# Hybrid decoder trunk: weight items of the up projection in two rings, each in the SBUF half of its operand

## The chip, the cores and the metric

The kernel runs on one core of one Trainium2 chip. The metric is the device time of one execution in microseconds. Engines are named as the profile names them: PE is TensorE (PEld its weight loads), DVE is VectorE, ACT is ScalarE, POOL is GpSimd, SP is SyncE.

## What is computed

Two layers over 1024 tokens of width 1024, all in fp32. Each layer has a token mixer of three parallel groups (latent attention, gated linear attention, RWKV-7) and a gated feed-forward part:

```python
for l in range(2):
    p = rms_norm(x) @ w_in
    y = concat[MLA(p_a), GLA(p_b), RWKV7(p_c)]            # width 1024
    x = x + y @ w_out
    u = rms_norm(x) @ w_up                                # 1024 -> 2 x 2816
    u = causal depthwise conv of width 3 over tokens (u) + bias
    gate, val = u[:, :2816], u[:, 2816:]
    x = x + (silu(gate) * val) @ w_down                   # 2816 -> 1024
out = rms_norm(x)
```

## The kernel before

**Products.** Every fp32 operand is split into two fp32r halves: hi is a copy on ACT, lo is the operand minus hi. One product of matrices is three matmuls (`mm3`, L99 to L102, all recorded at L97): hi by hi, hi by lo, lo by hi.

**Up projection.** The 2816 gate and 2816 value columns are taken in 22 blocks j of 128 each. A block is computed by a scheme of seven products instead of eight (p = 1, 2, 6, 5, 3, 7, 4 in this order, `seq`). Each product has four steps of `mm3`, so 12 matmuls of 128x512: the stationary operand is a weight item ("wr" in the profile: [128, 2, 4, 128], hi and lo, 4 KiB per partition), the moving one an activation operand of 512 tokens: B11 (p=1), B21 (2), B22 (3), T1 (5), T2 (6), T3 (7), T4 (4), 16 KiB per partition each. `rhs` picks it.

**Weight items.** `up_item` makes one item: for p=6 first four sums S of raw weights ("wu") on POOL, X and Y (L1364 to L1367), then `split`: the hi on ACT (L1271), the lo (L1272) on DVE for p = 2, 5, 7, 4 and on POOL for 1, 6, 3. Items lie in RING, seven slots; after product n item n+7 is made. A slot is written when the product that read it is done; a sum is overwritten when its readers are done.

**Evacuation.** `evac` takes a product out of PSUM (four banks, so product n needs the bank of n-4): p=1 and p=5 by ACT, the others by DVE (L1458 for p=2, L1460 for 6, L1465 for 3, L1479 for 7, L1471 for 4), with additions on POOL (L1466 gate, L1480 value). Then the convolution's taps: one on ACT (L1441), two on DVE (L1443), for gate and value; silu on ACT (L1468), the product of the two on DVE (L1475) and the store to `fdr`.

**SBUF.** Tiles are taken from two ends. The left end has the pool `slots` (m0 to m9, kb.., va.., sg, each 4 KiB; its names stand behind the tile's name in the profile, wr_m, T_kb), above 16 KiB of transfer scratch and the constants. The right end has the pools `wp` (ws, wh, wl), in the attention stage those of its tiles (v, p and others), later `xr` (x, raw) and `bp` (the five operands B11, B21, T2, T1, B22). T3 lies in `wp`. So before the change all weight items and T4 lie left, the six other operands right. A tile that takes the bytes of earlier tiles waits for their users.

**Output projection.** y is multiplied by w_out in eight k blocks, whose weights `wout_w` (L1158 to L1171) loads into "wos", splits by ACT (L1170) and, for k above 3, POOL (L1171). k=5, 6, 7 are split last; k=5 and 6 have slots of the left pool, k=7 has `wp`. The buffer of "wos" for these three is `wp`'s ws, two of them. The matmuls of a token tile go over k = 0 to 7. `up_norm` then makes the operands of the up projection for each of eight token tiles i.

**Down projection.** Its operands are loaded into the bytes of the up projection's operands (HOME) by `down_load`, from product p=1 of the last block on, and split into UNITS, nine pairs of buffers, by ACT and DVE.

**Order.** The program's order is that of the Python code, with background generators advanced by `spend`; the tile scheduler then orders each engine's queue by what is ready first in its own time line.

Of the kernel before, what the change touches and what calls it, by code (L numbers as in the profile page):

```python
# [10 lines left out]
F32 = mybir.dt.float32  # L11
F32R = mybir.dt.float32r
AF = mybir.ActivationFunctionType
ALU = mybir.AluOpType
# [47 lines left out]
def trunk(ctx: ExitStack, tc: tile.TileContext, A, out, offs):  # L62
# [241 lines left out]
    for l in range(DEPTH):  # L304
# [838 lines left out]
        def pv(h, i, pT, sm):  # L1143
            po = aps()
            for j in range(i + 1):
# [8 lines left out]
        WOA = (("m6", "m7"), ("m8", "m2"), ("m0", "m1"), ("va00", "va10"), ("kb00", "kb10"), ("kb01", "kb11"),  # L1154
               ("va01", "va11"))
        YA = (("m4", "m5"), ("sg", "m9"))

        def wout_w(k, ws=None):  # L1158
            if k < 7:
                woh[k], wol[k] = (slot(o, [128, D], F32R, "wo") for o in WOA[k])  # L1160
            else:
                woh[7], wol[7] = (wp.tile([128, D], F32R, tag="wl", name="wo7") for _ in range(2))
# [88 lines left out]
        bp = right.enter_context(tc.tile_pool(name=f"bp{l}", bufs=1, side="right", reuse_waits="tile"))  # L1251
        WU, WD = A["ffn_w_up"][l], A["ffn_w_down"][l]
# [8 lines left out]
        B11, B21, T2, T1, B22 = (pair(n) for n in ("B11", "B21", "T2", "T1", "B22"))  # L1261
# [11 lines left out]

        def up_norm(xt, i):
            raw = xr.tile([128, 8, 128], F32, tag="raw", name="raw")
# [25 lines left out]
            if i < 4:  # L1301
                split(at(B11), lo, dve)
                yield
                split(at(B21), hi, pool)
            else:
                for q in at(B11):
                    dve.tensor_tensor(lo, lo, q.bitcast(F32), ALU.subtract)
# [6 lines left out]
                for q in at(B11):  # L1314
                    dve.tensor_tensor(hi, hi, q.bitcast(F32), ALU.subtract)
# [4 lines left out]
        def late_sums():  # L1320
            for n, tags in enumerate((("m1", "kb00"), ("kb10", "kb01"))):
                r = slice(2 * n, 2 * n + 2)
                t = xr.tile([128, 2, 512], F32, tag="raw", name="ts")
# [17 lines left out]
        RING = ("m4", "m5", "sg", "m9", "m8", "kb11", "m3")  # L1341
# [12 lines left out]
        def up_item():  # L1354
            nonlocal rn
            if not todo:
                return
            j, p = todo.pop(0)
            g, v = (wraw[j] + [None])[0:2]
            eng = dve if j < SJ else pool  # L1360
            if p == 6:
                X = slot("va10", [128, 2, 4, 128], F32, "S12")
                Y = slot("va01", [128, 2, 4, 128], F32, "S34")
# [9 lines left out]
            c = slot(RING[rn % len(RING)], [128, 2, 4, 128], F32R, "wr")  # L1373
# [58 lines left out]
        def rhs(p, k):  # L1432
# [3 lines left out]
            a = {1: B11, 2: B21, 3: B22, 5: T1, 6: T2}[p]  # L1436
            return a[0][:, k], a[1][:, k]

        def taps(u, jj, tag):
            a = xr.tile([128, T], F32, **tag, name="acc")  # L1440
# [7 lines left out]
        def evac(j, p):  # L1448
# [3 lines left out]
            if p == 1:  # L1452
                tmp[j] = slot(("va00", "va11")[j % 2], [128, 3, 512], F32, "s")
                act.activation(tmp[j][:, 0], ps, AF.Copy)
# [260 lines left out]
```

## Time and profile before

| | us |
|---|---|
| median of 3 runs | 2757.17 |
| lowest, highest | 2750.89, 2757.83 |
| the profiled execution | 2754.38 |
| its span | 2752.6 |

The span is the stretch from the first to the last instruction in the profile; the profiled execution's own time is 1.8 us more. All times of the trace count from the span's start. Layer 2 follows layer 1 by 1370 us (the first w_out weight of the late three is split at 570.5 and at 1940.5). In layer 1 attention and RWKV last to about 595, the output projection to about 700, the up projection to about 1140, then comes the down projection.

### The profile page before, as it was taken

The page shows a single profiled execution, that of the slowest core. Times are in us where ns is not written, and L with a number is a line of the kernel's source. Part 1 is how long each engine was busy: PE and PEld are TensorE (multiplying, and loading weights), DVE is VectorE, ACT ScalarE, POOL GpSimd, SP SyncE. Part 2 cuts the span into 40 slices and gives each one's busy share as a digit, 9 for nine tenths or more (in the row PEclk, how much of TensorE's full clock was granted, in tenths as well). Part 3 has the DMA queues.
Part 4 walks back from the last instruction along what each step waited for, and adds up shares of the span by engine and source line. Part 5 has one row for each costly group of instructions (what it writes and reads, how often), then busy time and mean ns, then how long its engine had stood idle before and what let it go on. Part 6 is the DMA issues. An engine that isn't in the chain of part 4 may idle for free. (4 is left out here: it accounts for less than half of the span.)

```text
span 2752.6 us, 35450 instructions
## 1 busy us (share of the span) xinstructions
PE 2650.9 (96%) x13586; PEld 2135.5 (78%) x13586; DVE 1867.2 (68%) x2470; ACT 1080.8 (39%) x1764; POOL 1125.0 (41%) x915
## 2 busy tenths in 40 slices
PE   8999999999899999999899999999998999998998
PEld 7668788888778877778786777788887788776786
DVE  3456565645987777888733565555469887878887
ACT  4222244444434344433352223445544444443333
POOL 3446322232676666200134553222327767671001
PEclk9999989999999999999999999899999999999999
DMA  4112221134122222623111122111341222227221
GB/s 128 31 31 62 64 61 38 45 126 138 52 86 77 84 77 77 237 100 101 58 45 31 31 70 73 51 32 57 121 135 54 77 81 81 80 74 260 85 84 62
DMA packets 237050, 224.11 MB, mean 81 GB/s; under 512 B 39288, under 2 KB 187216, under 8 KB 236880
## 3 DMA queue, kind: packets, MB, share of 16 engines
q1 hardware_dynamic: 215104, 211.70, 23.8%
q10 hardware_dynamic: 21008, 8.04, 1.2%
q8 instruction: 107, 1.75, 0.3%
q0 software_dynamic: 768, 2.10, 0.2%
q14 instruction: 63, 0.52, 0.1%
HBM read 166.22 MB, written 53.48 MB: 80 GB/s over the span
## 5 line engine op out<-in xcount | busy, mean ns | idle before, releaser
L97 PE MATMUL psb<-hh,wh 128*128 128x512 f32 (+2 forms) x704 | 267.3, 381 | 6.5 <-ACT acc L748 3.8
L1443 DVE SCALAR_TENSOR_TENSOR acc<-ug,convc,acc 128x1023 f32<-128x1023 f32 x88 | 190.6, 2166 | 122.2 <-ACT acc L1441 122.1
L97 PE MATMUL psb<-hl,wh 128*128 128x512 f32 (+2 forms) x704 | 270.7, 385 | 0.8 <-DVE hl L208 0.8
L97 PE MATMUL psb<-hh,wl 128*128 128x512 f32 (+2 forms) x704 | 270.1, 384 | 0.8 <-POOL wl L258 0.8
L97 PE MATMUL psa<-B,wr_m 128*128 128x512 f32 x744 | 187.7, 402 | 1.9 <-DVE uv L1471 1.9
L97 PE MATMUL psr<-B,wr_m 128*128 128x512 f32 x744 | 185.6, 397 | 0.0
L97 PEld LDWEIGHTS psa<-B,wr_m 128*128 128x128 f32 x744 | 142.6, 192 | 37.5 <-DVE uv L1471 2.7
L254 POOL TENSOR_TENSOR ws<-ws,pcol 128x1024 f32<-128x1024 f32 x36 | 70.4, 1958 | 243.0 <-DMA ws<-in_w_in 242.8
L97 PEld LDWEIGHTS psr<-B,wr_m 128*128 128x128 f32 x744 | 140.6, 189 | 34.2 <-DVE s_va L1460 0.3
L97 PEld LDWEIGHTS psb<-hh,wh 128*128 128x128 f32 (+1 forms) x704 | 132.9, 189 | 36.5 <-issue 4.9
L97 PEld LDWEIGHTS psb<-hh,wl 128*128 128x128 f32 (+1 forms) x704 | 133.2, 189 | 33.3 <-issue 10.5
L97 PEld LDWEIGHTS psb<-hl,wh 128*128 128x128 f32 (+1 forms) x704 | 133.1, 189 | 29.2 <-issue 5.4
L258 POOL TENSOR_TENSOR wl<-ws,wh 128x1024 fp32r<-128x1024 f32 (+1 forms) x40 | 91.0, 2276 | 105.9 <-ACT wh L256 70.9
L1441 ACT ACTIVATE acc<-ug,convc 128x1024 f32<-128x1024 f32 x44 | 54.8, 1246 | 202.1 <-POOL ug L1466 202.1
L1443 DVE SCALAR_TENSOR_TENSOR acc<-uv,convc,acc 128x1023 f32<-128x1023 f32 x88 | 120.0, 1364 | 8.0 <-ACT acc L1441 6.7
L1272 DVE TENSOR_TENSOR wr_m<-wu_m,wr_m 128x512 fp32r<-128x512 f32 x88 | 120.9, 1375 | 0.2 <-ACT wr_m L1271 0.2
L1272 POOL TENSOR_TENSOR wr_sg<-S_va,wr_sg 128x512 fp32r<-128x512 f32 x40 | 58.0, 1449 | 120.0 <-ACT wr_sg L1271 116.3
L1468 ACT ACTIVATE acc<-acc 128x1024 f32<-128x1024 f32 x44 | 46.7, 1062 | 149.1 <-DVE acc L1443 149.1
L1271 ACT ACTIVATE de_m<-R 128x1024 fp32r<-128x1024 f32 x59 | 61.9, 1052 | 109.9 <-PE psb L97 50.8
L1364 POOL TENSOR_TENSOR S_va<-wu_m 128x512 f32<-128x512 f32 x42 | 57.0, 1358 | 114.8 <-issue 107.6
L256 ACT ACTIVATE wh<-ws 128x1024 fp32r<-128x1024 f32 (+2 forms) x44 | 43.7, 993 | 150.7 <-PE psb L97 141.4
L97 PE MATMUL psb<-de 128*128 128x512 f32 x348 | 94.6, 394 | 0.0
(534 smaller groups left out, 7119.0 us busy)
## 6 DMA issues: line engine op xcount, KB each, us to landing
wu_m<-in_ffn_w_up SPq DMA_DIRECT2D x88, 512.0 KB
fdr<-acc SPq DMA_DIRECT2D x44, 512.0 KB
R<-fdr SPq DMA_DIRECT2D x88, 256.0 KB
R<-in_ffn_w_down SPq DMA_DIRECT2D x88, 256.0 KB
ws<-in_w_in SPq DMA_DIRECT2D x38, 512.0 KB
y_m<-ydr SPq DMA_DIRECT2D x16, 512.0 KB
xmid<-x SPq DMA_DIRECT2D x16, 512.0 KB
wos_m<-in_w_out SPq DMA_DIRECT2D x10, 512.0 KB
```

Of the source, the lines that this page charges most:

```text
L97: pe.matmul(o, lhsT=l, rhs=r, start=first, stop=last, skip_group_check=on)
L254: eng.tensor_tensor(ws, ws, g.rearrange("p (k o) -> p k o", o=1).to_broadcast([128, K, M]), ALU.mult)
L256: act.activation(wh, ws, AF.Copy)
L258: eng.tensor_tensor(wl, ws, wh.bitcast(F32), ALU.subtract)
L1271: act.activation(d[0], s, AF.Copy)
L1272: eng.tensor_tensor(d[1], s, d[0].bitcast(F32), ALU.subtract)
L1364: eng.tensor_tensor(X[:, 0], v[:, 0:4], v[:, 4:8], ALU.add)
L1441: act.activation(a, u, AF.Identity, scale=conv[:, 2, jj:jj + 1], bias=conv[:, 3, jj:jj + 1])
L1443: dve.scalar_tensor_tensor(a[:, d:T], u[:, 0:T - d], conv[:, 2 - d, jj:jj + 1], a[:, d:T], ALU.mult, ALU.add)
L1468: act.activation(a, a, AF.Silu)
```

## The change

- Weight items get two rings: three slots on the left (m4, m5, sg) for p=1 and 4, five on the right (RG, 20 KiB in `bp`, at the place where B11 was) for p = 2, 3, 5, 6, 7. `up_item` is called twice after each product and makes an item only if its ring has a free place and at most seven are alive.
- B11 moves to the left: two pieces in kb01, kb11 and va01, va11. T4's second piece takes m3. So every product has weights and activations in the same half.
- Splits of B11 and subtractions of it (`less`) go in two halves of 256 columns each.
- w_out's k=5 and k=6 lose their slots to B11 and use the bytes of RG.
- The transfer scratch goes from 16 to 8 KiB; a pool `lp` (raw, ex) takes the room on the right. The tmp tiles of `evac` and X, Y get other slots on the left.
- Down projection: HOME is B21, T2, T1, B22, RG; the first loads come after p = 2, 6, 5 instead of 1, 2, 6; a tenth unit of operands "e" (raw, ex).

```diff
--- before.py
+++ after.py
@@ -1151,13 +1151,14 @@
         woh, wol, yy = [None] * 8, [None] * 8, {}
-        WOA = (("m6", "m7"), ("m8", "m2"), ("m0", "m1"), ("va00", "va10"), ("kb00", "kb10"), ("kb01", "kb11"),
-               ("va01", "va11"))
+        WOA = (("m6", "m7"), ("m8", "m2"), ("m0", "m1"), ("va00", "va10"), ("kb00", "kb10"))
         YA = (("m4", "m5"), ("sg", "m9"))
         def wout_w(k, ws=None):
-            if k < 7:
+            if k < 5:
                 woh[k], wol[k] = (slot(o, [128, D], F32R, "wo") for o in WOA[k])
+            elif k < 7:
+                woh[k], wol[k] = (RG[:, 2 * k - 10 + n].rearrange("p a k c -> p (a k c)") for n in range(2))
             else:
@@ -1249,6 +1250,7 @@
         bp = right.enter_context(tc.tile_pool(name=f"bp{l}", bufs=1, side="right", reuse_waits="tile"))
+        lp = right.enter_context(tc.tile_pool(name=f"lp{l}", bufs=1, side="right", reuse_waits="tile"))
         WU, WD = A["ffn_w_up"][l], A["ffn_w_down"][l]
@@ -1258,7 +1260,10 @@
 
-        B11, B21, T2, T1, B22 = (pair(n) for n in ("B11", "B21", "T2", "T1", "B22"))
+        RG = bp.tile([128, 5, 2, 4, 128], F32R, tag="RG", name="RG")
+        B21, T2, T1, B22 = (pair(n) for n in ("B21", "T2", "T1", "B22"))
+        B11 = [[slot(t, [128, 2, 512], F32R, "B11") for t in ts] for ts in (("kb01", "kb11"), ("va01", "va11"))]
         T4 = {}
@@ -1271,8 +1276,14 @@
 
+        def less(x, tk):
+            for part in B11:
+                for n in range(2):
+                    xn = x[:, 2 * n:2 * n + 2]
+                    dve.tensor_tensor(xn, xn, part[n][:, :, tk].bitcast(F32), ALU.subtract)
         def up_norm(xt, i):
-            raw = xr.tile([128, 8, 128], F32, tag="raw", name="raw")
+            raw = lp.tile([128, 8, 128], F32, tag="raw", name="raw")
             ss = cpool.tile([128, 2], F32, tag="ss", name="ss", bufs=2)
@@ -1299,28 +1310,27 @@
             if i < 4:
-                split(at(B11), lo, dve)
+                for n in range(2):
+                    split((B11[0][n][:, :, tk], B11[1][n][:, :, tk]), lo[:, 2 * n:2 * n + 2], dve)
                 yield
             else:
-                for q in at(B11):
-                    dve.tensor_tensor(lo, lo, q.bitcast(F32), ALU.subtract)
+                less(lo, tk)
                 split(at(B22), hi, pool)
                 split(at(T2), hi, dve)
-                for q in at(B11):
-                    dve.tensor_tensor(hi, hi, q.bitcast(F32), ALU.subtract)
+                less(hi, tk)
                 yield
         def late_sums():
-            for n, tags in enumerate((("m1", "kb00"), ("kb10", "kb01"))):
+            for n, tags in enumerate((("m1", "kb00"), ("kb10", "m3"))):
                 r = slice(2 * n, 2 * n + 2)
-                t = xr.tile([128, 2, 512], F32, tag="raw", name="ts")
+                t = lp.tile([128, 2, 512], F32, tag="raw", name="ts")
                 dve.tensor_tensor(t, B21[0][:, r].bitcast(F32), T2[0][:, r].bitcast(F32), ALU.subtract)
@@ -1338,7 +1348,9 @@
         seq += [(NF - 1, p) for p in (1, 2, 6, 5, 7, 4, 3)]
-        RING = ("m4", "m5", "sg", "m9", "m8", "kb11", "m3")
+        RING = ("m4", "m5", "sg")
+        live = [0, 0]
+        made = [0, 0]
         wraw, wsum, items, todo = {}, {}, {}, list(seq)
@@ -1353,14 +1365,18 @@
             nonlocal rn
-            if not todo:
+            if not todo or sum(live) > 6:
                 return
+            up = todo[0][1] not in (1, 4)
+            if live[up] == (3, 5)[up]:
+                return
+            live[up] += 1
             j, p = todo.pop(0)
             if p == 6:
-                X = slot("va10", [128, 2, 4, 128], F32, "S12")
-                Y = slot("va01", [128, 2, 4, 128], F32, "S34")
+                X = slot("m8", [128, 2, 4, 128], F32, "S12")
+                Y = slot("m9", [128, 2, 4, 128], F32, "S34")
                 eng.tensor_tensor(X[:, 0], v[:, 0:4], v[:, 4:8], ALU.add)
@@ -1370,7 +1386,9 @@
                 src = v[:, 4:8] if p == 4 else g[:, 0:4] if p == 1 else g[:, 4:8]
-            c = slot(RING[rn % len(RING)], [128, 2, 4, 128], F32R, "wr")
+            n = made[up]
+            c = RG[:, (n + 4) % 5] if up else slot(RING[n % 3], [128, 2, 4, 128], F32R, "wr")
+            made[up] += 1
             rn += 1
@@ -1433,11 +1451,13 @@
                 return a[0][:, k % 2], a[1][:, k % 2]
-            a = {1: B11, 2: B21, 3: B22, 5: T1, 6: T2}[p]
+            if p == 1:
+                return B11[0][k // 2][:, k % 2], B11[1][k // 2][:, k % 2]
+            a = {2: B21, 3: B22, 5: T1, 6: T2}[p]
             return a[0][:, k], a[1][:, k]
 
-        def taps(u, jj, tag):
-            a = xr.tile([128, T], F32, **tag, name="acc")
+        def taps(u, jj, pool_, tag):
+            a = pool_.tile([128, T], F32, **tag, name="acc")
             act.activation(a, u, AF.Identity, scale=conv[:, 2, jj:jj + 1], bias=conv[:, 3, jj:jj + 1])
@@ -1450,7 +1470,7 @@
             if p == 1:
-                tmp[j] = slot(("va00", "va11")[j % 2], [128, 3, 512], F32, "s")
+                tmp[j] = slot(("va10", "va00")[j % 2], [128, 3, 512], F32, "s")
                 act.activation(tmp[j][:, 0], ps, AF.Copy)
@@ -1464,12 +1484,12 @@
                 pool.tensor_tensor(u[:, H1], u[:, H1], s[:, 1], ALU.add)
-                a = tmp[j, "a"] = taps(u, j, dict(tag="x", bufs=2))
+                a = tmp[j, "a"] = taps(u, j, xr, dict(tag="x", bufs=2))
                 act.activation(a, a, AF.Silu)
                 dve.tensor_tensor(u[:, H0], ps, s[:, 0], ALU.add)
-                tmp[j, "b"] = taps(u, NF + j, dict(tag="raw"))
+                tmp[j, "b"] = taps(u, NF + j, lp, dict(tag="raw"))
             if {3, 4} <= done and p in (3, 4):
@@ -1489,6 +1509,7 @@
             c = items.pop((j, p))
+            live[p not in (1, 4)] -= 1
             for k in range(4):
@@ -1505,7 +1526,7 @@
             dtodo += [(q, p) for p in (1, "a", 2, 5, "b", 6, "c", 3, "d", 7, 4) for q in js]
-        HOME = ("B11", "B21", "T2", "T1", "B22")
+        HOME = ("B21", "T2", "T1", "B22", "RG")
         OPS = {1: (0, 4), 2: (1, 5), 5: (2, 6), 6: (2, 6), 7: (0, 4), 3: (1, 7), 4: (3, 5)}
@@ -1522,16 +1543,18 @@
 
-        UNITS = (("m6", "m7"), ("va10", "va01"), ("m4", "m5"), "w", ("m8", "kb11"), "w", ("sg", "m3"), "l", "x")
-        LEFT = [u for u in UNITS if u[0] not in "wlx"]
+        UNITS = (("kb11", "va01"), ("m6", "m7"), ("m4", "m5"), "w", ("m8", "va10"), "w", ("sg", "m3"), "l", "e", "x")
+        LEFT = [u for u in UNITS if u not in ("w", "l", "x")]
         late = len(groups[-1])
-        units = [UNITS[n % 9] for n in range(7 * NQ if l + 1 == DEPTH else 7 * NQ - 5 * late)]
-        units += [LEFT[n % 5] for n in range(7 * NQ - len(units))]
+        units = [UNITS[n % 10] for n in range(7 * NQ if l + 1 == DEPTH else 7 * NQ - 5 * late)]
+        units += [LEFT[n % 6] for n in range(7 * NQ - len(units))]
 
                 return tuple(xr.tile([128, 2, 512], F32R, tag="x", name="de", bufs=2) for _ in range(2))
+            if e == "e":
+                return tuple(lp.tile([128, 2, 512], F32R, tag=t, name="de") for t in ("raw", "ex"))
             if e in ("w", "l"):
@@ -1609,7 +1632,7 @@
 
-        for _ in range(len(RING) - 2):
+        for _ in range(5):
             up_item()
@@ -1618,10 +1641,11 @@
                 evac(2, 2)
-            up_item()
+            for _ in range(2):
+                up_item()
             if j == NF - 1:
-                if p in (1, 2, 6):
-                    down_load((1, 2, 6).index(p), (0, 4, 1, 5))
+                if p in (2, 6, 5):
+                    down_load((2, 6, 5).index(p), (0, 4, 1, 5))
                 if p == 5:
@@ -1700,7 +1724,7 @@
 
-    nc = bacc.Bacc("TRN2", target_bir_lowering=False, num_devices=1)
+    nc = bacc.Bacc("TRN2", target_bir_lowering=False, num_devices=1, dynamic_dma_scratch_size=8192)
     cst, offs, rope = _consts()
```

## Rows read from the trace of the kernel before

**Rows 1.** The page's first part: busy time (us), share of the span and instructions of each engine.
```profile
PE 2650.9 (96%) x13586; PEld 2135.5 (78%) x13586; DVE 1867.2 (68%) x2470; ACT 1080.8 (39%) x1764; POOL 1125.0 (41%) x915
```

**Rows 2.** Stretches (from:to, length), busy PE PEld DVE ACT POOL, PEclk, DMA share, GB/s.
```profile
690.00:780.00 90.00, 77.60 (x317) 60.95 (x316) 84.02 (x75) 38.13 (x59) 63.87 (x37) 0.92 0.20 65
780.00:1115.00 335.00, 334.92 (x1433) 267.88 (x1432) 263.37 (x238) 140.61 (x204) 225.60 (x153) 1.00 0.23 76
...
1140.00:1180.00 40.00, 31.96 (x113) 22.88 (x111) 40.00 (x46) 13.39 (x13) 3.11 (x2) 0.87 0.83 300
```

**Rows 3.** Timeline of PE, 901 to 924, up projection: start, duration, engine, line, operation, out<-in.
```profile
901.53 2.97 PE L97 MATMUL psa<-B,wr_m 128*128 128x512 f32 x12
...
918.39 0.39 PE L97 MATMUL psa<-T_m,wr_m 128*128 128x512 f32 x1
...
921.12 2.97 PE L97 MATMUL psr<-B,wr_m 128*128 128x512 f32 x12
...
923.92 2.97 PE L97 MATMUL psa<-B,wr_m 128*128 128x512 f32 x12
```

**Rows 4.** Timeline of PE, input projection of layer 2: first and last of 28 matmuls.
```profile
1429.71 0.39 PE L97 MATMUL psb<-hh,wh 128*128 128x512 f32 x1
...
1435.83 0.39 PE L97 MATMUL psb<-hh,wh 128*128 128x512 f32 x1
```

**Rows 5.** Timeline, 899 to 938: idle before it and its releaser in brackets.
```profile
899.07 1.30 POOL L1364 TENSOR_TENSOR S_va<-wu_m 128x512 f32<-128x512 f32 x1 [3.02 <-issue]
...
917.98 0.68 DVE L1272 TENSOR_TENSOR wr_m<-S_va,wr_m 128x512 fp32r<-128x512 f32 x1
...
918.79 1.30 POOL L1364 TENSOR_TENSOR S_va<-wu_m 128x512 f32<-128x512 f32 x1 [3.02 <-issue]
...
923.00 1.28 POOL L1466 TENSOR_TENSOR ug<-ug,s_va 128x512 f32<-128x512 f32 x1
...
924.32 1.25 ACT L1441 ACTIVATE acc<-ug,convc 128x1024 f32<-128x1024 f32 x1 [5.03 <-POOL ug L1466]
...
925.60 2.27 DVE L1443 SCALAR_TENSOR_TENSOR acc<-ug,convc,acc 128x1023 f32<-128x1023 f32 x1 [3.59 <-ACT acc L1441]
...
927.80 1.78 DVE L1272 TENSOR_TENSOR wr_m<-wu_m,wr_m 128x512 fp32r<-128x512 f32 x1
...
937.26 0.68 DVE L1460 TENSOR_TENSOR s_va<-psr,s_va 128x512 f32<-128x512 f32 x1
...
938.00 0.19 PEld L97 LDWEIGHTS psr<-T_m,wr_m 128*128 128x128 f32 x1 [0.31 <-DVE s_va L1460]
```

**Rows 6.** Timeline, 565 to 595: weights of the output projection (wos, wo), last pv.
```profile
565.95 1.36 SPq L1164 DMA_DIRECT2D wos<-in_w_out  x2
...
570.55 1.06 ACT L1170 ACTIVATE wo_kb<-wos 128x1024 fp32r<-128x1024 f32 x1 [0.30 <-DMA wos<-in_w_out]
...
574.00 2.36 POOL L1171 TENSOR_TENSOR wo_va<-wos,wo_va 128x1024 fp32r<-128x1024 f32 x1
...
574.07 0.33 SPq L1164 DMA_DIRECT2D wos<-in_w_out  x1
...
583.22 1.95 PE L1146 MATMUL psa<-v,pT 128*128 128x128 f32 x16
...
588.64 0.61 POOL L935 DMA_DIRECT2D ydr<-rcb  x1 [0.30 <-POOL rcb L934]
...
594.89 1.20 PE L97 MATMUL psr<-wo,yhl_m 128*128 128x512 f32 x4 [1.76 <-POOL wo L1171]
```

**Rows 7.** Timeline: a product after a long wait of PE.
```profile
770.21 5.46 PE L97 MATMUL psa<-T,wr_m 128*128 128x512 f32 x12 [4.90 <-DVE uv L1471]
```

**Rows 8.** Timeline, 662 to 666: subtractions of 512 and of 256 columns on DVE.
```profile
662.53 1.42 DVE L1315 TENSOR_TENSOR raw<-raw,B 128x512 f32<-128x512 f32 x2
...
664.73 0.76 DVE L1272 TENSOR_TENSOR T<-raw,T 128x256 fp32r<-128x256 f32 x2 [0.78 <-ACT T L1271]
```

**Rows 9.** Timeline: a wait of PE at the start of the down projection.
```profile
1158.95 1.22 PE L97 MATMUL psb<-de_m,de_m 128*128 128x512 f32 x2 [2.91 <-DVE de_m L1272]
```

## The prediction

> **What bounds the kernel now.** I read the page's first part, then the busy time by stage, then the lines of the up projection's stage, and last the lines around the start of the output projection. TensorE is busy 96% of the span and no other engine over 68% [rows 1], so one would take TensorE for the bound everywhere. By stage it is less simple [rows 2]: from 780 to 1115 TensorE is busy 334.92 of 335.00 us with VectorE at 263 and GpSimd at 226, while from 690 to 780, where the up projection starts, VectorE has 84 of 90 us, and from 1140 to 1180, where the down projection starts, 40.00 of 40.
>
> **The pace of a product.** Seven products of 12 matmuls (128x512) make one column block j. In [rows 3] p=1 starts at 901.53 and p=4 at 918.39: six products in 16.86 us, 2.81 each. p=4 itself takes 2.73 (918.39 to 921.12), the next one 2.80. Of the seven, p=4 alone has weights and activations both in the left half of SBUF; the six others meet a weight of the left with an activation of the right. That the half decides, and not the name, is borne out where both lie right: in the input projection 27 intervals between matmuls take 6.12 us, 227 ns each [rows 4], which is 2.72 for twelve. So same side 2.73, opposite sides 2.81. The six products of a j could give 6 x 0.08 = 0.48 us, and 44 blocks (22 in each of two layers) 21 us. The period of a j would go from 19.59 (901.53 to 921.12) to 19.11.
>
> **But there is a second chain with almost the same period, and TensorE isn't in it.** It is in [rows 5]. GpSimd's first sum (L1364) starts at 899.07 and 918.79: 19.72, longer than TensorE's 19.59. Follow it from 918.79: the sums and a lo, then GpSimd's L1466 (923.00), ScalarE's first tap (924.32, after 5.03 of idle, released by L1466), VectorE's taps (925.60, after 3.59 of idle, released by that), the lo of item 4 (927.80, 1.78 us, stretched while GpSimd runs), the rest of the taps, the evacuation L1460 (937.26), and then the lo of item 5, whose counterpart at 917.98 ended at 918.66: 0.13 later L1364 began, since that lo is the last reader of the sum it overwrites. So the loop L1364, L1466, taps, L1460, lo, L1364 closes through three engines. Up to 921.12 TensorE still runs at 19.59 and loses its lead to the loop bit by bit; at 938.00 it waits for L1460 (0.31), since a product needs the PSUM bank of four products before. "TensorE 99.98% busy" and "VectorE 79%" both hide this.
>
> **The change, part by part.**
> 1. *Weights on the operand's side.* TensorE's own work falls by 21 us. What of it is gained depends on the loop. The change doubles no sum, leaves sums, taps and evacuations on their engines, and the right-hand items, item 5 among them, still wait for the product that used their slot. It keeps items seven products ahead once j is over 2. Only left items (p=1 and 4) get a free slot earlier, so their lo can move in VectorE's and GpSimd's queues. My reading of the scheduler's order, which issues what is ready, is that the lo of item 4 moves from 927.80 to about L1460: still between L1466 and the lo of item 5, so within the loop; and GpSimd's work that now stretches it would stretch a tap instead. I take the loop as unchanged, 19.7. Then TensorE, at 19.11, meets it within two j and waits 0.6 us a j. Gain: the last j of each layer, which has no following sums, 0.5 each: **-1**. Bounds: -21 (loop open) to 0.
> 2. *w_out's k=5 and 6 in the weight ring.* Their old slots are free early: loads from 565.95, the hi at 570.55, the second lo 574.00 to 576.36, and the freed buffer takes k=7's load at 574.07 [rows 6]. The ring's bytes are those of attention tiles (v and p); its first write waits for the last matmul that reads v, which ends at 585.17 (583.22 + 1.95). The hi can then use ScalarE, but GpSimd has the RWKV tail until 589.25 (588.64 + 0.61). So k=5's lo runs 589.25 to 591.61, k=6's to 593.97. k=7's load starts at 591.61 instead of 574.07; a load takes 4.6 until its hi (565.95 to 570.55): 596.2, hi 1.06, lo 2.36: 599.6. TensorE had its last operand at 594.89, where it waited 1.76 for just this lo. So +4.7; downstream the work is TensorE's and then VectorE's chain, so nothing absorbs it. Two layers: **+9.4**. Bounds: 0 (the scheduler puts these splits where other work covers them) to +14.8, if TensorE's clock falls in the longer idle: after 4.90 us of waiting a product took 5.46 instead of 2.97 [rows 7], 2.5 more, per layer 2.7 with its neighbours.
> 3. *Those weights now lie opposite to y.* 2 weights x 2 halves x 8 token tiles x 3 = 96 matmuls per layer, 8 dozens at 0.08: **+1.3** in all. A bound of 0 if they fall into waits.
> 4. *Halved subtractions and splits.* Two of 512 columns take 1.42, two of 256 take 0.76 [rows 8], so four take 1.52: +0.1 each time. Most of it is before the last token tile and hidden by TensorE; what lies on the last tile's chain, where VectorE has 84 of 90 us [rows 2], is two such places and the split of the first operand: 0.4 per layer, **+0.8** (0 to +1.6).
> 5. *Items at the start.* The double call with limits (3 left, 5 right, 7 in all) keeps the order; in the first blocks the lead falls from 7 to 5 or 6. One item late costs its split at most, some 1.9 per layer; I take 0, as TensorE there waits for the last token tile and not for items.
> 6. *Down projection.* A tenth unit lets VectorE split one operand earlier. From 1140 to 1180 VectorE is full [rows 2], and TensorE's waits (2.91 for a lo [rows 9]) are for VectorE's pace, so another buffer helps little: **-2** over two layers (-4 to 0). First loads come one product later (2.8 us), when SP is still held by free buffers: **+0.5** (0 to 2).
> 7. *Smaller transfer scratch.* Nothing in the trace waits for it; 0, up to +0.6 (one GpSimd issue [rows 6]) per layer. Moved addresses of tmp, X and Y cost nothing: same number of slots, same readers.
>
> **Sum:** -1 + 9.4 + 1.3 + 0.8 - 2 + 0.5 = +9.0. The profiled execution took 2754.38 (span 2752.6), so 2763.4 there; it lies 2.8 under the median of 2757.17, so **2766** against that median.
>
> **A rule that speaks against the change.** The Trainium skill, "SBUF — State Buffer", section "SBUF: two separate sides", knows no left and right half for TensorE: within the engine side only the port pair shared by VectorE and GpSimd contends, and TensorE has ports of its own. By that rule the matmul term is 0 and the opposite placement of part 3 free too. The trace disagrees where it can be read: 2.73 against 2.81.
>
> **The rivals.**
> - *The loop opens* (27%). If the scheduler puts the lo of item 4 behind the lo of item 5, it falls into VectorE's idle time before the taps (3.59 us [rows 5]), and the loop loses up to 1.78 us, more than the 0.6 needed. Then TensorE runs at 19.11: -21 + 10 of the other parts = -11, **2746**. For it: the freed slot makes that lo movable at all. Against: item 5's lo becomes ready only after its own product, later than item 4's would. It decides where 0.6 us a j leaves the loop; between, the gain is 44 times what leaves it.
> - *The loop gets longer* (11%). Item 1's lo on GpSimd, its left slot now free a product earlier, is issued ahead of L1466 at 923.00. Price 1.3 us a j (a GpSimd operation of 512 columns, as L1364 takes 1.30 [rows 5]) over some 18 j per layer: +47 + 9, **2813**. It decides once item 1's hi is done before 923.00. Against: ScalarE's queue has that hi behind the first tap now.
> - *The halves decide nothing* (5%): p=4 is quicker for another reason, its two-piece operand for instance, and all products stay at 2.81. Then +9.0 + 1 - 1.3 = **2766**, the same time by another way. Against: [rows 4].
> - The forecast (57%): loop unchanged, w_out's tail paid for.
>
> **How the numbers follow.** A measurement of this kernel tells about 0.3%, 8.3 us, from no change. The forecast's own range is 2757 (the w_out term hidden) to 2777 (half clock twice, late items); about half of it lies over +8.3. Faster: most of the open loop and some cases between: 0.26. Slower: half the forecast, the long loop, half the third rival: 0.38. Same: 0.36. The range takes in the open loop with 4 us below it and the forecast's upper end: 2743 to 2779; left out are the long loop and the ends.
>
> **What would show it.** Right: all seven products start 2.73 apart where nothing waits, yet p=1 starts come 19.7 apart; TensorE's idle before p=4 or p=1, released by VectorE's L1460 or L1458, grows to some 0.6 a j; TensorE's share from 780 to 1115 falls to 97%. The lo of k=5 and 6 (L1171) near 589 to 594, k=7's near 597 to 600, and TensorE waiting about 5 us more there. Wrong: L1364 at 19.1 to 19.3 apart (open loop), at 20 or more (long loop), products still at 2.81 (halves decide nothing), k=7's lo at 593 (w_out term is 0), or a shorter or longer 690 to 780 than 90 us by more than 2.

## The result

Medians of seven runs each: 2770.24 us after (2766.84 to 2777.57) against 2754.52 before (2747.91 to 2760.19). The ratio is 1.0056, with a 95% interval of 1.0041 to 1.0070: slower, by 15.7 us between the medians. The profiled execution of the changed kernel has a span of 2768.5 us, 15.9 more than that of before. Two executions in the experiments took 3689.60 and 5157.39 us, far above the others of their kernels, and are left out of every median below; the second of them was the profiled one, so the trace of that kernel (the w_out edits alone) is not read.

First the page's first part and the busy time of three stretches, columns as in [rows 1, 2]:

```profile
PE 2646.1 (96%) x13586; PEld 2139.1 (77%) x13586; DVE 1839.8 (66%) x2510; ACT 1082.8 (39%) x1772; POOL 1176.6 (43%) x915
...
690.00:780.00 90.00, 77.28 (x320) 62.13 (x319) 84.40 (x85) 38.71 (x60) 62.51 (x36) 0.92 0.24 72
780.00:1115.00 335.00, 328.95 (x1426) 265.87 (x1425) 250.67 (x239) 139.59 (x203) 247.48 (x155) 1.00 0.24 77
...
1140.00:1180.00 40.00, 34.27 (x131) 26.16 (x129) 36.38 (x43) 15.44 (x15) 2.97 (x2) 0.87 0.86 314
```

In the up projection TensorE is now busy 328.95 of 335 us instead of 334.92: it does nearly the same number of matmuls (1426 and 1433) in less time and waits for the rest. The timeline of one block of the changed kernel, TensorE's products and the lines that close the chain (as in [rows 3, 5]; its lines stand 16 to 20 further down: L1380 is the old L1364, L1486 the old L1466, L1461 and L1463 the taps, L1277 a lo, L1480 the old L1460, L1478 the old L1458, L1491 the old L1471):

```profile
907.30 1.29 POOL L1380 TENSOR_TENSOR S_m<-wu_m 128x512 f32<-128x512 f32 x1 [3.02 <-issue]
...
911.50 1.28 POOL L1486 TENSOR_TENSOR ug<-ug,s_va 128x512 f32<-128x512 f32 x1
...
912.19 2.92 PE L97 MATMUL psr<-B,RG 128*128 128x512 f32 x12
...
912.82 1.25 ACT L1461 ACTIVATE acc<-ug,convc 128x1024 f32<-128x1024 f32 x1 [5.51 <-POOL ug L1486]
...
914.10 2.28 DVE L1463 SCALAR_TENSOR_TENSOR acc<-ug,convc,acc 128x1023 f32<-128x1023 f32 x1 [4.96 <-ACT acc L1461]
914.95 2.88 PE L97 MATMUL psa<-T,RG 128*128 128x512 f32 x12
...
916.31 0.68 DVE L1491 TENSOR_TENSOR uv<-psr,s_va 128x512 f32<-128x512 f32 x1
...
917.67 2.88 PE L97 MATMUL psr<-T,RG 128*128 128x512 f32 x12
...
920.39 2.88 PE L97 MATMUL psa<-B,RG 128*128 128x512 f32 x12
...
920.78 0.68 DVE L1277 TENSOR_TENSOR wr_sg<-wu_m,wr_sg 128x512 fp32r<-128x512 f32 x1
...
923.31 2.59 PEld L97 LDWEIGHTS psr<-T,RG 128*128 128x128 f32 x12 [0.46 <-DVE ug L1478]
...
925.42 0.68 DVE L1480 TENSOR_TENSOR s_va<-psa,s_va 128x512 f32<-128x512 f32 x1
...
926.02 0.68 DVE L1277 TENSOR_TENSOR RG<-S_m,RG 128x512 fp32r<-128x512 f32 x1
...
926.15 0.19 PEld L97 LDWEIGHTS psa<-T_m,wr_m 128*128 128x128 f32 x1 [0.24 <-DVE s_va L1480]
...
926.83 1.30 POOL L1380 TENSOR_TENSOR S_m<-wu_m 128x512 f32<-128x512 f32 x1 [3.02 <-issue]
...
931.74 2.92 PE L97 MATMUL psa<-B,RG 128*128 128x512 f32 x12
```

Products that wait for nothing start 2.72 us apart (914.95, 917.67, 920.39), where they had 2.81 [rows 3]. But p=2 comes 19.55 after the last p=2 (912.19 to 931.74) and L1380 19.53 after the last L1380, against 19.72 [rows 5]: the same chain through GpSimd's sum, its addition, the taps and the lo of item 5 (926.02), 0.13 after whose end L1380 starts again. Before p=7 and p=4 the weight loads wait for VectorE. This is the shorter of two kinds of block: of the 32 steady blocks of the two layers 24 take 19.49 to 19.54 by L1380, and 8 take 20.12 to 20.17 (the last section shows why). Their mean is 19.67, against 19.75 for the same blocks before.

**Where the time went.** I laid the n-th matmul of one trace beside the n-th of the other (13586 in both) and read how far the changed kernel lags:

| stretch (us of before) | lag grows by |
|---|---|
| up to 556, where the change touches only the scratch's size | +0.6 |
| start of the output projection, 556 to 625 | +5.2 |
| rest of it, to 684 | +0.5 |
| start of the up projection, to 782 | +1.3 |
| its blocks, to 1133 | -0.9 |
| down projection, into layer 2 | -0.9 |
| layer 2: start of the output projection, 1945 to 1998 | +8.2 |
| rest of it, to 2058 | +0.3 |
| up projection, start and blocks, to 2495 | +0.3 |
| down projection, to the last matmul | -2.4 |
| after the last matmul | +3.8 |

But for rounding they add up to the 15.9. Within the first stretch alone the lag moves from -0.9 (at 370) to +0.6 (at 390), so a row of 1 us tells little. The start of the output projection, the lines that answer to [rows 6] (L1171 makes the hi, L1172 the lo):

```profile
582.33 3.51 PE L1146 MATMUL psa<-v,pT 128*128 128x128 f32 x30
...
587.67 2.00 ACT L1171 ACTIVATE RG<-wos 128x1024 fp32r<-128x1024 f32 x2
...
588.81 4.72 POOL L1172 TENSOR_TENSOR RG<-wos,RG 128x1024 fp32r<-128x1024 f32 x2 [1.87 <-ACT RG L1171]
...
591.22 0.33 SPq L1165 DMA_DIRECT2D wos<-in_w_out  x1
...
594.58 1.06 ACT L1171 ACTIVATE wo<-wos 128x1024 fp32r<-128x1024 f32 x1 [4.92 <-DMA wos<-in_w_out]
...
595.72 2.35 POOL L1172 TENSOR_TENSOR wo<-wos,wo 128x1024 fp32r<-128x1024 f32 x1 [2.19 <-ACT wo L1171]
...
598.12 2.07 PE L97 MATMUL psr<-wo,yhl_m 128*128 128x512 f32 x4 [1.70 <-POOL wo L1172]
...
598.00:606.00 8.00, 7.88 (x22) 5.84 (x23) 1.87 (x3) 3.21 (x6) 1.58 (x5) 0.62 0.22 73
```

The ring's bytes are written only after the last matmul on v; then lo, load, hi and lo follow one another. The last row is the stretch behind it: TensorE's mean granted clock is 0.62 of its 2.4 GHz, after a chain of short waits, so part of it ran at 1.2.

The last stretch is new too. In the timeline of the end, ScalarE waits 10.41 us for one accumulator while finished ones stand in line behind it. After TensorE's last matmul (2754.00) twelve of the last scalings on VectorE (L1710, the old L1686) are left, five before the change:

```profile
2750.11 0.63 ACT L218 ACTIVATE o<-acc_m 128x512 f32<-128x512 f32 x1 [10.41 <-DVE acc_m L1627]
...
2754.00 0.39 PE L97 MATMUL psb<-de_sg,de_m 128*128 128x512 f32 x1
```

### The profile page after: what moved, and what is told of

Same layout as the page of the kernel before. It is cut to its first block, busy times and chain, and to the rows that moved or that the text cites. A ratio compares the mean times of both kernels' runs of the same rounds, so it can differ in the third digit from the quotient of the medians.

```text
span 2768.5 us, 35437 instructions
## 1 busy us (share of the span) xinstructions
PE 2646.1 (96%) x13586; PEld 2139.1 (77%) x13586; DVE 1839.8 (66%) x2510; ACT 1082.8 (39%) x1772; POOL 1176.6 (43%) x915
## 5 line engine op out<-in xcount | busy, mean ns | idle before, releaser
L1463 DVE SCALAR_TENSOR_TENSOR acc<-ug,convc,acc 128x1023 f32<-128x1023 f32 x88 | 173.7, 1973 | 176.2 <-ACT acc L1461 176.1
L97 PE MATMUL psr<-T,RG 128*128 128x512 f32 x840 | 214.0, 405 | 25.9 <-ACT T L1276 10.8
L97 PEld LDWEIGHTS psr<-T,RG 128*128 128x128 f32 x840 | 163.0, 196 | 67.1 <-ACT T L1276 11.7
L97 PE MATMUL psa<-T,RG 128*128 128x512 f32 x744 | 181.4, 392 | 9.1 <-DVE ug L1478 9.0
L1277 POOL TENSOR_TENSOR RG<-S_m,RG 128x512 fp32r<-128x512 f32 x86 | 148.7, 1729 | 68.2 <-ACT RG L1276 66.9
L97 PEld LDWEIGHTS psa<-T,RG 128*128 128x128 f32 x744 | 138.6, 188 | 44.0 <-DVE ug L1478 15.7
L1463 DVE SCALAR_TENSOR_TENSOR acc<-uv,convc,acc 128x1023 f32<-128x1023 f32 x88 | 165.9, 1885 | 3.6 <-ACT acc L1461 3.4
L1276 ACT ACTIVATE RG<-S_m 128x512 fp32r<-128x512 f32 x176 | 106.1, 625 | 142.2 <-PE psa L97 73.9
L1461 ACT ACTIVATE acc<-ug,convc 128x1024 f32<-128x1024 f32 x44 | 54.8, 1245 | 216.9 <-POOL ug L1486 216.8
L258 POOL TENSOR_TENSOR wl<-ws,wh 128x1024 fp32r<-128x1024 f32 (+1 forms) x40 | 91.1, 2280 | 99.9 <-ACT wh L256 65.0
L1276 ACT ACTIVATE de<-R 128x1024 fp32r<-128x1024 f32 x67 | 68.9, 1053 | 161.2 <-PE psb L97 59.7
L97 PE MATMUL psa<-B,RG 128*128 128x512 f32 x528 | 128.0, 391 | 0.0
L97 PE MATMUL psr<-B,RG 128*128 128x512 f32 x504 | 122.4, 391 | 0.0
L1380 POOL TENSOR_TENSOR S_m<-wu_m 128x512 f32<-128x512 f32 x42 | 63.6, 1514 | 137.2 <-issue 127.6
```

The source lines that it names most:

```text
L97: pe.matmul(o, lhsT=l, rhs=r, start=first, stop=last, skip_group_check=on)
L258: eng.tensor_tensor(wl, ws, wh.bitcast(F32), ALU.subtract)
L1276: act.activation(d[0], s, AF.Copy)
L1277: eng.tensor_tensor(d[1], s, d[0].bitcast(F32), ALU.subtract)
L1380: eng.tensor_tensor(X[:, 0], v[:, 0:4], v[:, 4:8], ALU.add)
L1461: act.activation(a, u, AF.Identity, scale=conv[:, 2, jj:jj + 1], bias=conv[:, 3, jj:jj + 1])
```

## The experiments

The theory from the two traces: the matmuls gain 0.45 to 0.5 us a block, and a loop of GpSimd, ScalarE and VectorE takes it back; the loss comes from w_out's start and the end. The rivals: the halves give nothing, or VectorE is the bound and not the loop. Each kernel below is compared with the kernel before as measured beside it (medians of 2755.43 to 2756.35).

**1. Open the loop.** In both kernels the gate's addition goes from GpSimd to VectorE:

```diff
-                pool.tensor_tensor(u[:, H1], u[:, H1], s[:, 1], ALU.add)
+                dve.tensor_tensor(u[:, H1], u[:, H1], s[:, 1], ALU.add)
```

> The kernel before with the same addition (L1466) given to VectorE. Theory: with the loop open TensorE's own pace shows, six products at 2.81 and one at 2.73: blocks at 19.59, against 19.71 before, so only 1 to 5 us less than before (2750 to 2754). The difference between this and the changed kernel with the same edit is then what the halves are worth: 0.48 us a block. Rival (the halves give nothing): the two kernels with the edit have the same period of a block.

> The changed kernel with the gate addition (L1486, GpSimd) given to VectorE, so that the first taps no longer wait behind GpSimd's sums. Theory (a loop through GpSimd's sums, that addition, the taps and the lo of item 5 gives back what the matmuls gain): the loop opens, the blocks of the up projection come 19.1 to 19.2 us apart instead of 19.5 to 20.2, the up stage loses some 0.5 us a block, and the time falls by 15 to 22 us against the changed kernel, to about 2750. Rival (the halves give nothing, TensorE's own pace is 2.8 a product): blocks at 19.5 to 19.7, time within 4 us of the changed kernel's 2770. Rival (VectorE or its contention with GpSimd is the bound, not the loop): blocks at 19.5 or longer, since VectorE gets one more addition, time the same or longer.

Measured: the kernel before with the edit 2740.53 against 2755.93, ratio 0.9943 (0.9931 to 0.9955); the changed kernel with it 2760.28, ratio 1.0014 (1.0005 to 1.0023). First the timeline of TensorE in the former, two starts of p=1; then, in the latter, a lo on GpSimd, the lo of item 4 and two waits before p=7 in layer 1, and two starts of p=1 with the lo of item 4 between them in layer 2:

```profile
1017.67 2.97 PE L97 MATMUL psa<-B,wr_m 128*128 128x512 f32 x12
...
1037.26 2.97 PE L97 MATMUL psr<-B,wr_m 128*128 128x512 f32 x12
```

```profile
956.47 1.49 POOL L1277 TENSOR_TENSOR RG<-S_m,RG 128x512 fp32r<-128x512 f32 x1 [0.74 <-ACT RG L1276]
956.73 1.78 DVE L1277 TENSOR_TENSOR wr_m<-wu_m,wr_m 128x512 fp32r<-128x512 f32 x1
...
960.36 2.63 PEld L97 LDWEIGHTS psr<-T,RG 128*128 128x128 f32 x12 [0.54 <-DVE ug L1478]
...
979.91 2.60 PEld L97 LDWEIGHTS psa<-T,RG 128*128 128x128 f32 x12 [0.49 <-DVE ug L1478]
...
2302.59 0.39 PE L97 MATMUL psr<-B_kb,wr_m 128*128 128x512 f32 x1
...
2309.85 0.68 DVE L1277 TENSOR_TENSOR wr_m<-wu_m,wr_m 128x512 fp32r<-128x512 f32 x1
...
2321.73 0.39 PE L97 MATMUL psa<-B_kb,wr_m 128*128 128x512 f32 x1
```

With the loop open the old kernel runs at 19.59 a block (1017.67 to 1037.26), the changed one in layer 2 at 19.14 (2302.59 to 2321.73). That is TensorE's own pace in both, and the halves are worth 0.45 us a block; the rival that they give nothing falls. But layer 1, with the same order of instructions, ran at 19.55 (960.36 to 979.91), TensorE waiting for L1478. So there is a second chain. It runs over VectorE and ScalarE, and whether it closes seems to hang on how long VectorE's work takes beside GpSimd's: the lo of item 4 takes 1.78 in layer 1 and 0.68 in layer 2. Both sizes were wrong: the changed kernel gained 10 us where 15 to 22 were expected, the old one 15 where 1 to 5 were. By the n-th matmul the old kernel's steady blocks gained 1.5 and 1.0 us in the two layers, as thought; the starts of the up projection (to the sixth block) gained 3.1 and 3.6 and the starts of the down projection 3.5 and 4.4 more, the start of layer 2's output projection lost 4.2, and stretches that the edit doesn't touch moved by up to 2.3. By which wait the starts gained was not followed, so of the 15 us only some 2.5 are shown to be the loop's.

**2. Open it without more work for VectorE.** GpSimd adds the two stored products of the gate, so that its addition need not wait for p=3:

```diff
             elif p == 5:
                 act.activation(s[:, 1], ps, AF.Copy)
+                u = tmp[j, "g"]
+                pool.tensor_tensor(u[:, H1], s[:, 2], s[:, 1], ALU.add)
@@
-                dve.tensor_tensor(u[:, H1], ps, s[:, 2], ALU.add)
-                pool.tensor_tensor(u[:, H1], u[:, H1], s[:, 1], ALU.add)
+                dve.tensor_tensor(u[:, H1], ps, u[:, H1], ALU.add)
```

> The kernel before; GpSimd adds the two stored products of the gate (s2 and s1) before p=3 is done, and VectorE adds that sum to p=3: same number of additions, none of them between p=3 and the first taps, VectorE gets nothing extra. Theory (the loop ran through that GpSimd addition): loop open, blocks at 19.59 (TensorE's pace on opposite sides), starts of the two stages shorter as with the addition on VectorE; 2736 to 2745, 10 to 19 us less than before. Rival (VectorE had gained only by taking work off GpSimd): blocks at 19.7, time within 4 us of before.

> The same edit in the changed kernel. With the addition on VectorE layer 2 ran at 19.14 a block and layer 1 at 19.55, the same order of instructions, so two patterns of contention between VectorE and GpSimd. Theory (the loop, and the stretching of VectorE's work beside GpSimd's, decide; TensorE's own pace is 19.1): without the extra addition on VectorE both layers run at 19.1 to 19.2, time 2742 to 2752, some 20 to 28 us less than the changed kernel and 3 to 11 less than with the addition on VectorE. Rival (19.55 is a second loop that this edit doesn't touch): one or both layers at 19.5, time within 4 us of 2760.

Measured: the old kernel 2744.30, ratio 0.9953 (0.9941 to 0.9966), blocks 19.59 apart, both as expected. The starts of the down projection gained 4.3 and 4.4 us, but those of the up projection, which were to gain too, lost 0.4 and 0.5. The changed kernel 2773.29, ratio 1.0058 (1.0046 to 1.0070): a miss. Its timeline, the second chain over one block and TensorE's wait for it:

```profile
944.36 2.59 PEld L97 LDWEIGHTS psa<-T,RG 128*128 128x128 f32 x12 [0.84 <-DVE ug L1478]
...
946.79 1.61 POOL L1484 TENSOR_TENSOR ug<-s_va 128x512 f32<-128x512 f32 x1 [4.82 <-DVE s_va L1480]
...
948.43 0.69 DVE L1487 TENSOR_TENSOR ug<-psr,ug 128x512 f32<-128x512 f32 x1 [1.19 <-POOL ug L1484]
...
950.44 1.54 DVE L1463 SCALAR_TENSOR_TENSOR acc<-ug,convc,acc 128x1023 f32<-128x1023 f32 x1 [1.32 <-ACT acc L1461]
...
958.24 2.43 DVE L1463 SCALAR_TENSOR_TENSOR acc<-uv,convc,acc 128x1023 f32<-128x1023 f32 x1 [1.72 <-ACT acc L1461]
...
960.59 1.78 DVE L1277 TENSOR_TENSOR wr_m<-wu_m,wr_m 128x512 fp32r<-128x512 f32 x1
...
964.22 2.60 PEld L97 LDWEIGHTS psr<-T,RG 128*128 128x128 f32 x12 [0.85 <-DVE ug L1478]
```

One block takes 19.86 (944.36 to 964.22). VectorE waits three times (1.19, 1.32, 1.72) for the others' steps between its own, and the lo of item 4 stands behind the first value tap, where it hides in no wait. The first chain was opened, the second closes at 19.9. The edit itself lengthened it: the moved addition (L1484) waits for L1480, the evacuation of p=6, so VectorE's first wait, 1.19, is for a GpSimd step that now lies in the second chain. The form of the theory in which one loop decides falls: the first chain closes at 19.5 in the changed kernel, the second at 19.55 in experiment 1 and at 19.86 here.

**3. Take item 4's lo out of the second chain.** As in 1, and `LD = (2, 5, 7)` instead of `(2, 5, 7, 4)`, so that GpSimd makes that lo.

> The changed kernel with the gate addition on VectorE and the lo of item 4 on GpSimd. The traces so far show a second chain of 19.5 to 19.9 us a block, on VectorE: evacuation of p=4, ScalarE's tap of the value half (1.7 us of waiting), a tap, the lo of item 4 (1.78, beside GpSimd's work), a tap, evacuation of p=2, for which TensorE waits. Theory (that lo, which the change moved from VectorE's wait for ScalarE's tap to behind the first value tap, closes the second chain): without it both layers come to TensorE's pace, 19.1 to 19.2 a block, and the time to 2742 to 2750, some 10 to 18 us less than with the addition alone. Rival (VectorE and GpSimd contend for as long whoever makes that lo): 19.4 or more in one layer at least, time within 5 us of 2760.

> The same two edits in the kernel before. TensorE is the bound there already with the addition alone (19.59 a block). Theory: still 19.59, time within 4 us of that kernel's 2740; the difference from the changed kernel with the same edits is 0.45 us a block. Rival (the halves give nothing): both kernels have the same period.

Measured: the changed kernel 2756.17, ratio 0.9994 (0.9984 to 1.0004); the old one 2747.86, ratio 0.9961 (0.9947 to 0.9975). Waits before p=7 in the changed kernel, 19.38 and 19.41 apart, and two starts of p=1 in the old one, 19.59 apart:

```profile
940.41 2.59 PEld L97 LDWEIGHTS psa<-T,RG 128*128 128x128 f32 x12 [0.33 <-DVE ug L1478]
...
959.79 2.63 PEld L97 LDWEIGHTS psr<-T,RG 128*128 128x128 f32 x12 [0.29 <-DVE ug L1478]
...
979.20 0.76 PEld L97 LDWEIGHTS psa<-T,RG 128*128 128x128 f32 x4 [0.32 <-DVE ug L1478]
```

```profile
1005.03 2.97 PE L97 MATMUL psr<-B,wr_m 128*128 128x512 f32 x12
...
1024.62 2.97 PE L97 MATMUL psa<-B,wr_m 128*128 128x512 f32 x12
```

Both layers of the changed kernel are better than 19.5, and no 19.1: the work beside GpSimd stretches other steps instead. The expectation of 10 to 18 us was too high; the gain of 4 is the rival's (within 5 us of 2760), and its 19.4 a block is nearly met too. The old kernel stays at TensorE's 19.59, so the halves bring 0.2 a block here. Its time missed: 2747.86 where within 4 us of 2740 was expected. By the n-th matmul the starts of its up projection gained 1.2 and 1.2 us, where experiment 1 had 3.1 and 3.6. Its profiled execution lay 5.3 us behind before 556 us, where nothing differs, so from it I read periods and no sum of the whole.

**4. The start of the output projection.** k=7 loads into a free buffer, and VectorE makes the lo of k=5 and 6:

```diff
-            ws = slot("m9", [128, D], F32, "wos") if k < 5 else wp.tile([128, D], F32, tag="ws", name="wos")
+            if k == 7:
+                ws = lp.tile([128, D], F32, tag="ex", name="wos")
+            else:
+                ws = slot("m9", [128, D], F32, "wos") if k < 5 else wp.tile([128, D], F32, tag="ws", name="wos")
@@
-                pool.tensor_tensor(wol[k], ws, woh[k].bitcast(F32), ALU.subtract)
+                (dve if k in (5, 6) else pool).tensor_tensor(wol[k], ws, woh[k].bitcast(F32), ALU.subtract)
```

> The changed kernel, with the w_out weights of k=7 loaded into the buffer ex, so that the load doesn't wait for the lo of k=5, and the lo of k=5 and 6 made on VectorE instead of GpSimd. The weights stay in the ring's bytes and still wait for the last matmul that reads v. Theory (the start of the output projection costs 5.3 us in layer 1 and 8.2 in layer 2, by that wait and by the load and splits behind it): TensorE's last operand comes at 594 to 596 in layer 1 instead of 598.1, no half clock behind it, time 5 to 11 us less than the changed kernel, about 2762. Rival (this delay is absorbed further down, by the VectorE-bound start of the up projection): time within 3 us of the changed kernel.

> Both edits in the changed kernel. Theory: the parts add, 2738 to 2748, faster than the kernel before by 0.3 to 0.7%. Rival: either edit's gain is lost downstream and the time stays within 4 us of the better single edit.

> The same edit and the two edits on the w_out weights together in the changed kernel. Theory: another 5 to 7 us less than with the early sum alone, 2736 to 2746. Against the kernel before with the early sum it is what remains of the change: 0.45 us a block won (some 16 us), w_out's start (some 6), the tail (3.8) and what the down projection gains (3.5): within 10 us of it, either way.

> The changed kernel with the addition on VectorE, the lo of item 4 on GpSimd and the two edits on the w_out weights. Theory: the best of the changed kernels, 5 to 7 us less than without the w_out edits, 2735 to 2744, so faster than the kernel before by 0.4 to 0.8%, and within 6 us of the kernel before with the addition on VectorE, since w_out's start (some 6 left), and the tail (3.8) take back most of the 16 us that the halves give.

| the changed kernel with | without the w_out edits, us | with them, us | ratio with them |
|---|---|---|---|
| no other edit | 2770.24 | 2765.32 | 1.0036 (1.0023 to 1.0049) |
| the addition on VectorE | 2760.28 | 2754.31 | 0.9991 (0.9983 to 1.0000) |
| the early sum | 2773.29 | 2768.39 | 1.0037 (1.0024 to 1.0049) |
| addition and item 4's lo moved | 2756.17 | 2755.50 | 0.9995 (0.9986 to 1.0003) |

The timeline of the second kernel with the edits:

```profile
590.09 2.35 DVE L1175 TENSOR_TENSOR RG<-wos,RG 128x1024 fp32r<-128x1024 f32 x2
...
594.34 2.34 POOL L1175 TENSOR_TENSOR wo<-wos,wo 128x1024 fp32r<-128x1024 f32 x1 [6.25 <-ACT wo L1174]
...
596.73 2.08 PE L97 MATMUL psr<-wo,yhl_m 128*128 128x512 f32 x4 [1.70 <-POOL wo L1175]
```

Its run stood 1.1 us behind the changed kernel's at the last matmuls on v's side (556 us), and the last operand still came 1.4 us earlier, 596.73 instead of 598.12. That is less than expected (594 to 596), and the lower clock stayed, though shorter: from 590 to 606 the mean granted clock is 0.89 instead of 0.79. In three of the four pairs the edits give 5 to 6 us, so the delay of w_out's start is not all absorbed downstream. In the fourth they give 0.7, less than the runs scatter. The traces of the last three pairs agree on the place: by the n-th matmul the two starts of the output projection come 5.7, 6.3 and 7.9 us shorter. In the fourth pair 2.5 us of that are gone by the end of the start of layer 1's up projection, and 2.8 in layer 2's down projection; why is open. The three sums expected with both edits (2738 to 2748, 2736 to 2746 and 2735 to 2744) all missed, by 6 to 22 us: they stood on blocks near TensorE's own 19.1. The rest of the cost, the wait for the last matmul on v, stays with the bytes that were chosen; other bytes were not tried. No version of the changed kernel comes to the old one with the addition on VectorE.

**5. The tenth unit.** The changed kernel with `UNITS` without "e", and its counts back to 9 and 5:

> The changed kernel with nine operand units in the down projection instead of ten (the pair raw and ex is left out). The trace of the changed kernel shows 3.5 us less in the down projection of the two layers and 3.8 us more after the last matmul. If the tenth unit is what gains: time 2 to 4 us more than the changed kernel. If the gain comes from the other order of loads: time the same. If the longer tail (more squares and stores left after the last matmul) comes from the order that the tenth unit brings: up to 4 us less.

Measured: 2767.25, ratio 1.0035 (1.0023 to 1.0047), so it lies 11.0 us over the kernel before beside it, where ten units lay 15.7 over theirs. Its last matmul starts 11.9 us behind that of before, as with ten units (12.1), and the span ends 11.9 behind, where the changed kernel ends 15.9 behind. So the tenth unit gained nothing here: the down projections gain 3.4 us in all by the n-th matmul, 3.3 with ten, and the long tail is not there. The order in which the scheduler puts the last squares came with it.

**6. The scratch alone**, 8 KiB in the kernel before:

> The kernel before with the transfer scratch at 8 KiB instead of 16, nothing else (the left tiles move 8 KiB down, each stays in its half). Theory (nothing waits for the scratch): time within 4 us of the kernel before, blocks of the up projection at 19.7 as before. Rival (fewer descriptors hold up GpSimd's transfers of the RWKV results, 16 in a layer): up to 0.6 us each, 10 us a layer, seen in the stretch before 595 us.

Measured: 2757.76, ratio 1.0007 (0.9996 to 1.0017): nothing, as expected. Its blocks come 19.7 apart by L1364, as before.

## Why the prediction was right

The time forecast was 2766 and is 2770.2, slower, by the mechanism forecast: TensorE's gain per product came (2.72 for 2.81) and a chain without TensorE gave it back. As a difference the forecast was further off: +9.0, where +15.7 was measured. The kernel before ran at 2754.52 beside it, 2.7 under the median that the forecast stands on, and it is luck that this brought the times closer.

- *The up projection, -1.* Blocks: -0.9 in layer 1, +0.3 in layer 2 together with its start. Right. That the loop binds can be read off the block above, where no step of it starts more than 0.2 us after the one before it ends. Experiment 1 bears it out in layer 2, which runs at 19.14 without it; in layer 1 the second chain took its place, and that chain the prediction didn't have. The lo of item 4 moved within the loop, as I had thought, though to between the two value taps (920.78) and not to L1460. The loop is not unchanged: it came to 19.52 from 19.71, with 20.15 in 8 of 32 blocks. The lo takes 0.68 in it instead of 1.78, but L1491 (916.31), which lay outside it as L1471, lies inside now; what each is worth was not taken apart. The mean of 19.67 is 0.6 more than seven products at 2.72, the 0.6 a j that was forecast, though the waits are before p=7 and p=4 where I had named p=4 or p=1. TensorE's share from 780 to 1115 is 98% (forecast 97%).
- *w_out's k=5 to 7, +9.4.* The order and the times of layer 1 held: lo at 588.8 and 591.2 (forecast 589.3 and 591.6), k=7's last operand at 598.1 (599.6, as the load took 3.4 and not 4.6), and then a stretch at the lower clock. The first of these is right by luck: GpSimd's RWKV tail, which was to set it, ended at 586.94, and the lo waited 1.87 for its hi on ScalarE. Mis-sized was layer 2, which I had taken for a copy of layer 1: 5.2 + 8.2 = 13.4. In layer 2 of before TensorE had k=7 done 6.0 us after its last matmul on v (1961.64 to 1967.62), in layer 1 10.9 (585.17 to 596.09). In the changed kernel the same stretch takes 13.1 in layer 2 (1967.40 to 1980.52) and 14.4 in layer 1 (585.84 to 600.19): a chain that starts at that matmul costs more where less lay behind it.
- *Opposite sides, +1.3:* 0.5 + 0.3. *Halved subtractions and splits at the start, +0.8:* 1.3 in layer 1 and, with the blocks, 0.3 in layer 2. Both small and of the right sign, and within what untouched code moves by, so neither is shown.
- *Down projection, -1.5 in all:* -0.9 and -2.4, but by experiment 5 not through the tenth unit. That step was right by its sum alone.
- *Left out:* the end, +3.8. I had priced the unit and not what another order does to the last squares.
- *The rivals.* The open loop didn't come by itself: item 4's lo didn't go behind that of item 5. The halves do decide something, and a two-piece operand is not what makes a product quicker: T2 and T1, in one piece on the right, take 2.72 now (914.95 to 917.67 to 920.39). Which property of the addresses counts was not tried; moving the left tiles by 8 KiB changed nothing (experiment 6). The long loop, item 1's lo ahead of L1486, didn't come; 19.86 came in experiment 2, by another chain.

The rule of the Trainium skill, "SBUF — State Buffer", section "SBUF: two separate sides", that TensorE's ports never wait on anyone, knows no left and right half, so by it the placement would be free. It isn't here: the change moved operands between halves, kept the matmuls, and a product that was on opposite sides came down by 0.09 us, from 2.81 to 2.72. What it waited for on opposite sides, no row shows.

## What to carry to other kernels

Before a gain on the busiest engine is booked, follow the buffers of one period around through the other engines: a loop whose period is within 1% of that engine's is the next bound, even where the profile shows the engine 99.9% busy. Then look for the chain behind it, too: opening the first loop here only brought up a second one. Moving one addition off the first chain made the old kernel 0.5 to 0.6% faster, most of it at the starts of the stages and not in the steady blocks, while the better placement, with what it costs elsewhere, won nothing. A resource that looks free in the stage where it is used (the ring's bytes) is paid for where its bytes were used before, once for each place, and each place has to be read by itself.

## What the runs showed of the hardware

VectorE and GpSimd, started within 0.03 us of one another, can come out either way. VectorE's last value tap and GpSimd's lo in the changed kernel, in one block and two blocks later (timeline):

```profile
862.20 2.41 DVE L1463 SCALAR_TENSOR_TENSOR acc<-uv,convc,acc 128x1022 f32<-128x1022 f32 x1
862.23 1.30 POOL L1277 TENSOR_TENSOR RG<-S_m,RG 128x512 fp32r<-128x512 f32 x1 [1.63 <-ACT RG L1276]
...
901.87 1.27 DVE L1463 SCALAR_TENSOR_TENSOR acc<-uv,convc,acc 128x1022 f32<-128x1022 f32 x1
901.90 2.38 POOL L1277 TENSOR_TENSOR RG<-S_m,RG 128x512 fp32r<-128x512 f32 x1 [1.64 <-ACT RG L1276]
```

One of the two takes its 1.3 us and the other 1.1 longer. In all 32 steady blocks of the two layers the 8 in which VectorE's tap is held (2.39 to 2.41) are the 8 that take 20.12 to 20.17, and the 24 in which it takes 1.27 or 1.28 are those at 19.49 to 19.54. The same page of the Trainium skill, same section, calls the port pair of the two a lock held for a whole instruction, and these rows agree. It gives the pair to the one that starts first; here VectorE's start is the earlier by 0.03 us in both rows, and it got the pair in one of them only, so at this distance no row here tells beforehand which gets it.

The two patterns of experiment 1 (19.55 and 19.14, one order of instructions) show such a meeting too: the lo of item 4 takes 1.78 beside a lo on GpSimd that started 0.26 us earlier (956.47), and 0.68 in layer 2 (2309.85), where that one starts at 2311.48. What puts a layer into one pattern or the other is not shown. With the w_out edits the same blocks ran at 19.55 in both layers, so a period read in one layer or kernel need not hold in the other.
